# Loads of x issued two weight units apart, and a product of reciprocals that waits three units, in a hybrid encoder layer

## The chip, the cores and the metric

The kernel runs on one core of one Trainium2 chip. The metric is the device time of one execution in microseconds (us). Five engines run side by side, each in its own program order: TensorE (PE) multiplies matrices, VectorE (DVE) and ScalarE (ACT) work elementwise, GpSimd (POOL) takes a few additions, and SyncE (SP) issues most of the transfers (DMAs). An engine goes past an instruction only when the semaphores that it waits for have come.

## The reference

One encoder layer over x, 256 rows by 2048 columns in float32. Only its first steps matter here:

```python
h = rms_norm(x, norm1_g[i])       # x * rsqrt(mean(x*x) + eps) * g
proj = h @ w_in[i]                # 2048 x 20032: SSD z, xBC, dt | q, k, v | GLU | gates
y_ssd  = ssd_mixer(proj[..., COL_Z:COL_XBC], ..., dt = proj[..., COL_DT:COL_Q], ...) @ w_ssd_o[i]
y_att  = dilated_attention_mixer(q, k, v, q_norm_g[i], k_norm_g[i]) @ w_attn_o[i]   # q, k: RMSNorm per head
y_conv = conformer_conv(...) @ w_conv_o[i]
merged = sum over branches of sigmoid(gate) * y
x = x + merged @ w_out[i]
x = x + square(relu(rms_norm(x, norm2_g[i]) @ w_mlp_up[i])) @ w_mlp_down[i]
```

In the SSD branch `dt = softplus(dt_raw + dt_bias)`, and the decays are sums over the rows of `dt * a`.

## The kernel before

The weights are streamed once. They are cut into **blocks** (one output tile `main` each) and a block into **units** of 256 weight rows, mostly 8 to a block. For each unit the kernel loads the weights (`raw`, on SP's queue, five buffers), splits them into a high part `hi` (ACT, L1211) and a remainder `lo` (DVE, L255), and multiplies: high by high, high by the remainder of the activations, and `lo` by high (L1273, L1274, L1276 in one layout, L1264, L1266, L1268 in the other). In the program's order, loads stand five units ahead of the products (`load(k + 5)`), splits three (`LEAD`).

Units are counted from 0 here. Units 0 to 7 are block 0 (64 columns of dt and 384 of q), 8 to 15 block 1 (384 of k), 16 to 23 block 2 (384 of v). These three multiply `xg`, which is x times the gain, without the row's norm: the factor 1/rms is put on afterwards. From block 3 (unit 24, the first GLU block) on, the products use `h`, so they need `hh` and `hl`, the split of x times gain times 1/rms. There are two `main` tiles, so block n+2 may begin only once block n has been read.

Everything else is a set of **jobs**, Python generators that yield what they need, and a planner that puts their instructions between the units while it writes the program. `("w", n)` lets n units go by; `("v", cost)`, `("a", cost)`, `("p", cost)` ask for time on DVE, ACT and PE; `("m", n)` and `("b", n)` take buffers; `("j", test)` waits for another job. Priorities go from 0, the most urgent. After each unit, `tick` lets the jobs go on as far as their credits reach. Where a block needs something that isn't there yet, `require` forces the jobs, with no regard to credits and waits. From `mm` and from `Sched.require`:

```python
S.require(lambda: id(j) in st["main_free"], f"block {bi - 2} read")   # at the first unit of block bi
...
level = 0
while not cond():
    moved = False
    for j in [x for x in self.jobs if x.prio <= level]:
        while not cond() and not j.done and self._try(j, True):
            moved = True
```

What is forced is written ahead of the first product of the block that asked. The level rises only when no job of the lower levels can move.

The jobs of the first blocks:

- `job_rms1` (priority 0, added ahead of unit 3): loads x in its natural layout as four tiles `xr` of 512 KB (L318), sums the squares of each (ACT, L325), adds them up and takes the reciprocal of the root (`rstd_steps`: ACT L270, DVE L273 to L283) into `r`; `st["r1"]` then lets other jobs use it. `spread` puts `r` on a diagonal `dg` (DVE, L291), and a product with ones (PE, L296) spreads it over the partitions; DVE copies it to `rbc` (L338).
- `job_h` (priority 1): waits for `rbc`, and makes `hf`, `hh`, `hl` in four steps (DVE L354, ACT L357, DVE L255).
- `job_qk` (priority 0) for q of block 0 and k of block 1: squares of the heads (ACT, L459), then with `r` the norm of the heads (L469 to L482), the scaled copy `qn` (ACT, L489), transposes (PE, L501) and a copy out (ACT, L505, L506). For block 0, `main` counts as read only once this job has made `qn` and `job_dt` has read its columns.
- `job_dt` (priority 1) for block 0: waits for `r`, scales its 64 columns (DVE, L386), permutes the rows by a product (PE, L395), computes softplus as absolute value, exponential (ACT, L403, L404) and a series of small operations (DVE, L408 to L424), then a product that adds up the decays (PE, L436).

`job_rms2`, the second norm, also calls `spread`.

Of the kernel before, what the change touches and what calls it, by code (L numbers as in the profile page):

```python
# [190 lines left out]
def kernel(ctx: ExitStack, tc: tile.TileContext, xT, xn, par, cm, cd, cq, w1, wq, ws, out):  # L191
# [17 lines left out]
    def slab(shape, dt=F32, name="s"):  # L209
        return gp.tile([P] + list(shape), dt, tag="g", name=nm(name))  # L210

    def bank(shape=(512,), name="b"):
        return pd.tile([P] + list(shape), F32, tag="d", name=nm(name))

    def small(shape, name, dt=F32, bufs=None):
        return sm.tile([P] + list(shape), dt, tag=name, name=nm(name), bufs=bufs)
# [30 lines left out]
    def natural(ap):  # L247

        return ap.rearrange("p (j r) -> p r j", r=2)

    def strided(ap):
        return ap.rearrange("p (r j) -> p r j", r=2)
# [12 lines left out]
    def rstd_steps(dst, ms, n):  # L265

        s = small([n], f"rs{n}", bufs=2 if n < 64 else 1)
        r = small([n], f"rr{n}", bufs=2 if n < 64 else 1)
        yield "a", 1500 + n
        A.activation(s, ms, AF.Sqrt)  # L270
        yield "w", 1
        yield "v", (100 if n == T else 800) + 7 * n
        V.reciprocal(r, s)  # L273
        for b_ in (r, ms):
            if n == T:
                yield "v", 200 + n
            V.tensor_tensor(s, r if b_ is r else s, b_, op=ALU.mult)
        if n == T:
            yield "v", 200 + n
        V.tensor_scalar(s, s, -0.5, 1.5, op0=ALU.mult, op1=ALU.add)  # L280
        if n == T:
            yield "v", 200 + n
        V.tensor_tensor(dst, r, s, op=ALU.mult)  # L283

    def spread(r):

        yield "m", 1
        dg = slab([2, P], name="dg")
        yield "v", 400
        for t in range(2):  # L290
            V.tensor_scalar(dg[:, t, :], ID, r[:, t:t + 1], None, op0=ALU.mult)  # L291
        yield "w", 1
        yield "b", 1
        b = bank()
        yield "p", 440
        PE.matmul(b[:, :T], ones, dg, start=True, stop=True)  # L296
        S.give()
        yield "w", 1
        return b[:, :T]
# [10 lines left out]
    def job_rms1():  # L310

        xss = small([2, 2], "xss1", bufs=1)
        yield "m", 4
        xs_ = []
        for t in range(2):
            for e in range(2):
                xr = slab([1024], name="xr")
                nc.sync.dma_start(xr, xn.rearrange("(p t) d -> p t d", t=2)[:, t, e * 1024:e * 1024 + 1024])  # L318
                xs_.append(xr)
        yield "w", 2  # L320
        for t in range(2):
            for e in range(2):
                yield "a", 1300
                xr = xs_[2 * t + e]
                A.activation(xr, xr, AF.Square, accum_out=xss[:, t, e:e + 1])  # L325
        S.give(4)
        yield "w", 1
        m2 = small([2], "ms2", bufs=2)
        yield "v", 300
        V.tensor_reduce(m2, xss, axis=AX.X, op=ALU.add)  # L330
        V.tensor_scalar(m2, m2, 1.0 / D, EPS, op0=ALU.mult, op1=ALU.add)
        r2 = cp.tile([P, 2], F32, name="r2")
        yield from rstd_steps(r2, m2, 2)
        st["r1"] = r2
        b = yield from spread(r2)
        rbc = small([T], "rbc", bufs=1)
        yield "v", 400
        V.tensor_copy(natural(rbc), strided(b))  # L338
        S.banks += 1
        st["rbc1"] = rbc  # L340
# [676 lines left out]
    def job_rms2():  # L1017
        xss = small([2, 4], "xss", bufs=1)
        for i in range(4):
            yield "j", lambda: oacc[i] is not None  # L1020
            yield "m", 1
            sq = slab([2, 512], name="sq2")
            for t in range(2):
                yield "a", 650
                A.activation(sq[:, t, :], oacc[i][:, t, :], AF.Square, accum_out=xss[:, t, i:i + 1])
            S.give()
        ms = small([2], "ms2", bufs=2)
        yield "w", 1
        yield "v", 250
        V.tensor_reduce(ms, xss, axis=AX.X, op=ALU.add)  # L1030
        V.tensor_scalar(ms, ms, 1.0 / D, EPS, op0=ALU.mult, op1=ALU.add)
        r = small([2], "ry", bufs=1)
        yield from rstd_steps(r, ms, 2)
        b = yield from spread(r)
        rb = small([T], "rbc", bufs=1)
        yield "a", 300
        A.activation(rb, b, AF.Copy)
        S.banks += 1
        st["rbc2"] = rb
# [61 lines left out]
    def start_jobs():  # L1101
        S.add(job_rms1(), "rms1", 0)
# [298 lines left out]
```

## Time and profile before

| | |
|---|---|
| time, median of 3 runs | 1983.57 us (1982.33 to 1984.44) |
| the profiled execution: time | 1982.2 us |
| its span, first to last instruction | 1980.4 us |
| mean granted TensorE clock | 0.998 of full |
| PE busy | 1965.4 us (99% of the span) |
| DVE, ACT, POOL busy | 66%, 52%, 2% |
| HBM read | 360.45 MB, 183 GB/s over the span |

A row of the timeline gives start, duration, engine, line and operation, output from input, count, and in brackets the idle time ahead of it with what ended it. Busy PE time counts the ends of pipelined products, so the spacing of starts tells the pace. In the group rows stand count, total busy us, mean ns, and the engine's idle time before them. Names in the profile leave out the buffer numbers.

### The profile page before, as it was taken

What the parts mean: (1) busy time and instruction counts of PE and PEld (TensorE: products, weight loads), DVE (VectorE), ACT (ScalarE), POOL (GpSimd) and SP (SyncE); (2) the same over time, 40 slices, a digit from 0 to 9 for tenths busy, and PEclk for the clock granted to TensorE, in tenths of its full rate; (3) what the DMA queues carried; (4) which work ended last, traced back from release to release, by engine and by line L of the source; (5) the groups of instructions that cost most, each with busy time, mean ns of one, the idle gap of its engine ahead of it and who ended that gap; (6) DMA issues with size and microseconds to landing.
All of it is one profiled execution on the core that took longest, in us unless ns stands there. A gap on an engine that the chain in (4) does not pass through costs nothing.

```text
span 1980.4 us, 29949 instructions
## 1 busy us (share of the span) xinstructions
PE 1965.4 (99%) x11798; PEld 1766.0 (89%) x11798; DVE 1309.1 (66%) x1847; ACT 1036.5 (52%) x1446; POOL 47.4 (2%) x42
## 2 busy tenths in 40 slices
PE   8999999999999999999999999999999999999999
PEld 7999999999998888888888888999988998998887
DVE  5778987887887889896655555555555554455443
ACT  6555576777756655545654444544443443354332
POOL 0000010000000000003000000000000000000000
PEclk9999999999999999999999999999999999999999
DMA  8555564554555555555555556555555555555554
GB/s 289 184 173 190 163 186 142 169 173 141 180 169 167 174 181 181 181 191 186 188 190 189 184 193 207 195 183 190 192 190 189 186 191 191 190 185 190 191 181 149
DMA packets 105342, 364.51 MB, mean 184 GB/s; under 512 B 11760, under 2 KB 12272, under 8 KB 105200
## 3 DMA queue, kind: packets, MB, share of 16 engines
q1 hardware_dynamic: 103904, 360.23, 55.4%
q10 hardware_dynamic: 1296, 2.36, 0.3%
q8 instruction: 92, 1.51, 0.3%
q14 instruction: 50, 0.41, 0.1%
HBM read 360.45 MB, written 2.10 MB: 183 GB/s over the span
## 4 chain that ended last, share of the span: by engine, by line
PE 95%; DVE 0%; issue 0%
PE main L1273 19%; PE main L1274 19%; PE main L1276 19%; PE main L1266 11%; PE main L1264 11%; PE main L1268 11%; PE b L842 1%; PE b L864 1%; PE b L968 1%; PE b L1273 0%; PE b L1274 0%; PE b L1276 0%; PE b L819 0%; PE b L501 0%; PE b L757 0%; PE b L685 0%
## 5 line engine op out<-in xcount | busy, mean ns | idle before, releaser
L255 DVE TENSOR_TENSOR lo<-raw,hi 128x1024 fp32r<-128x1024 f32 (+2 forms) x697 | 831.5, 1194 | 643.7 <-ACT hi L1211 638.5
L1211 ACT ACTIVATE hi<-raw 128x1024 fp32r<-128x1024 f32 (+2 forms) x695 | 716.1, 1032 | 868.7 <-PE main L1274 487.0
L1273 PE MATMUL main<-hi,hh 128*128 128x512 f32 (+1 forms) x800 | 306.1, 383 | 0.0
L1274 PE MATMUL main<-hi,hl 128*128 128x512 f32 (+1 forms) x800 | 299.0, 374 | 0.0
L1266 PE MATMUL main<-x2l,hi 128*128 128x256 f32 x1024 | 246.4, 281 | 0.0
L1264 PE MATMUL main<-x2h,hi 128*128 128x256 f32 x1024 | 246.3, 279 | 0.0
L1266 PE MATMUL main<-hl,hi 128*128 128x256 f32 x896 | 216.3, 281 | 3.2 <-DVE hl L255 3.2
L1264 PE MATMUL main<-hh,hi 128*128 128x256 f32 x896 | 217.7, 282 | 0.0
L565 DVE SCALAR_TENSOR_TENSOR co<-cin,cpar,co 128x256 f32<-128x256 f32 x480 | 211.1, 491 | 0.0
L1276 PE MATMUL main<-lo,hh 128*128 128x512 f32 (+1 forms) x800 | 200.5, 372 | 0.0
L1264 PEld LDWEIGHTS main<-x2h,hi 128*128 128x128 f32 x1024 | 192.7, 188 | 0.2
L1266 PEld LDWEIGHTS main<-x2l,hi 128*128 128x128 f32 x1024 | 192.6, 188 | 0.2
L1273 PE MATMUL main<-hi,ah 128*128 128x512 f32 x480 | 188.9, 394 | 0.0
L1274 PE MATMUL main<-hi,al 128*128 128x512 f32 x480 | 188.6, 393 | 0.0
L1273 PEld LDWEIGHTS main<-hi,hh 128*128 128x128 f32 x800 | 152.5, 191 | 23.3 <-ACT hi L1211 1.2
L1274 PEld LDWEIGHTS main<-hi,hl 128*128 128x128 f32 x800 | 152.2, 190 | 22.9 <-issue 1.9
L1266 PEld LDWEIGHTS main<-hl,hi 128*128 128x128 f32 x896 | 168.8, 188 | 4.2 <-DVE hl L255 3.6
L1264 PEld LDWEIGHTS main<-hh,hi 128*128 128x128 f32 x896 | 169.2, 189 | 0.6
L1276 PEld LDWEIGHTS main<-lo,hh 128*128 128x128 f32 x800 | 148.0, 190 | 22.1
L1268 PE MATMUL main<-x2h,lo 128*128 128x256 f32 x1024 | 138.3, 277 | 0.0
L1276 PE MATMUL main<-lo,ah 128*128 128x512 f32 x480 | 130.1, 393 | 0.0
L1268 PEld LDWEIGHTS main<-x2h,lo 128*128 128x128 f32 x1024 | 127.6, 188 | 0.0
(244 smaller groups left out, 2303.8 us busy)
## 6 DMA issues: line engine op xcount, KB each, us to landing
raw<-ws_dram SPq DMA_DIRECT2D x600, 512.0 KB, 3.3
raw<-wq_dram SPq DMA_DIRECT2D x88, 384.0 KB, 3.1
raw<-w_dram SPq DMA_DIRECT2D x7, 448.0 KB, 7.1
xr<-xn_dram SPq DMA_DIRECT2D x4, 512.0 KB, 8.5
x<-xn_dram SPq DMA_DIRECT2D x4, 512.0 KB, 4.4
xt<-xT_dram SPq DMA_DIRECT2D x7, 256.0 KB, 7.2
out_dram<-x SPq DMA_DIRECT2D x4, 256.0 KB, 3.7
out_dram<-x ACTq DMA_DIRECT2D x4, 256.0 KB, 5.6
```

What stands on the lines that cost most here:

```text
L255: V.tensor_tensor(lo, raw, hi.bitcast(F32), op=ALU.subtract)
L565: V.scalar_tensor_tensor(dst[:, e, :], x[:, e, k:k + T], par_("dw", (2 * i + e) * 31 + k), dst[:, e, :], op0=ALU.mult, op1=ALU.add)
L842: PE.matmul(ba, lt, src, start=(n == 0), stop=(n == 3))
L864: PE.matmul(bd[:, i, :], em[:, 0, i, :], x[:, c, pr:pr + P], start=True, stop=True)
L968: PE.transpose(b[:, e, t * P:t * P + P], src[:, t, k * P:k * P + P], ID)
L1211: A.activation(h, r, AF.Copy)
L1264: PE.matmul(o, wh[:, e, cs], ah, start=(first and e == 0 and c % 2 == 0), stop=False, skip_group_check=True)
L1266: PE.matmul(o, wh[:, e, cs], al, start=False, stop=False, skip_group_check=True)
L1268: PE.matmul(o, wl[:, e, cs], ah, start=False, stop=(last and e == 1), skip_group_check=True)
L1273: PE.matmul(o, ah[:, xs_], wh[:, e, :], start=(first and e == 0), stop=False)
L1274: PE.matmul(o, al[:, xs_], wh[:, e, :], start=False, stop=False)
L1276: PE.matmul(o, ah[:, xs_], wl[:, e, :], start=False, stop=(last and e == 1))
```

## The change

In `job_rms1`, `yield "w", 2` stands after each of the four loads of x, where there was none; the wait of two units behind the loop stays. `spread` gets a parameter for the wait between the diagonal and its product, 1 as before by default, and 3 in the first norm. Lines below the edit move down by one.

```diff
-    def spread(r):
+    def spread(r, wait=1):
...
-        yield "w", 1
+        yield "w", wait
...
                 xs_.append(xr)
+                yield "w", 2
         yield "w", 2
...
-        b = yield from spread(r2)
+        b = yield from spread(r2, 3)
```

What the planner makes of it shows in the order of each engine's instructions. First SP's queue, where the loads of x meet the weight loads; `raw_228` is unit 8's weights, and the next `raw` rows are units 9, 10 and so on. Before:

```order
L1193 DMA raw_228<-wq_dram 128x768
L318 DMA xr_254<-xn_dram 128x1024
L318 DMA xr_256<-xn_dram 128x1024
L318 DMA xr_258<-xn_dram 128x1024
L318 DMA xr_260<-xn_dram 128x1024
L1193 DMA raw_262<-wq_dram 128x768
L1193 DMA raw_284<-wq_dram 128x768
```

The same place now:

```order
L1194 DMA raw_228<-wq_dram 128x768
L318 DMA xr_254<-xn_dram 128x1024
L1194 DMA raw_256<-wq_dram 128x768
L1194 DMA raw_278<-wq_dram 128x768
L318 DMA xr_296<-xn_dram 128x1024
L1194 DMA raw_298<-wq_dram 128x768
L1194 DMA raw_316<-wq_dram 128x768
L318 DMA xr_334<-xn_dram 128x1024
L1194 DMA raw_345<-wq_dram 128x768
L1194 DMA raw_378<-wq_dram 128x768
L318 DMA xr_396<-xn_dram 128x1024
```

The four loads of x stood in a row ahead of unit 9's weights; now two weight loads stand between each pair, and the last comes ahead of unit 15's.

Second, PE around the spread product (`dg` by ones, L296). Before, it stood between units 10 and 11, with `job_dt`'s first product behind it; `lo_326` is unit 10's remainder and `hi_356` unit 11's high part:

```order
L1276 MATMUL main_360<-lo_326,xgh_99 128x384 x4
L296 MATMUL b_430<-dg_405,ones 128x256
L395 MATMUL b_436<-dtt_342,perm_343 128x128 x4
L1273 MATMUL main_360<-hi_356,xgh_99 128x384
L1274 MATMUL main_360<-hi_356,xgl_102 128x384
```

Now it stands between unit 15 (`lo_437`) and unit 16 (`hi_454`, the first product into `main_679`, block 2):

```order
L1277 MATMUL main_354<-lo_437,xgh_101 128x384 x4
L296 MATMUL b_531<-dg_528,ones 128x256
L502 MATMUL b_590<-cmask,qn_582 128x128 x4
L502 MATMUL b_591<-cmask,qn_582 128x128 x2
L396 MATMUL b_639<-dtt_336,perm_337 128x128 x4
L437 MATMUL b_668<-adt,cmask 128x128 x4
L1274 MATMUL main_679<-hi_454,xgh_98 128x384
```

Four kinds of product moved to this one place: the spread product, the transposes of k's heads (`qn_582`; before they stood ahead of block 3), and `job_dt`'s permutation and its sums of decays (`adt`; before in block 4).

Third, ACT at the same place; `hi_511` is unit 19's split, `main_169` block 0, `main_354` block 1, `qn_549` q's heads. It read, before, from the first root on:

```order
L270 ACTIVATE rs_62_377<-ms_61_373 128x2
L1211 ACTIVATE hi_384<-raw_323 128x768
L459 ACTIVATE junk_381,ss_380<-main_169 128x128
L1211 ACTIVATE hi_414<-raw_351 128x768
L459 ACTIVATE junk_381,ss_380<-main_169 128x128 x4
L1211 ACTIVATE hi_443<-raw_382 128x768
L459 ACTIVATE junk_381,ss_380<-main_169 128x128
L1211 ACTIVATE hi_473<-raw_412 128x768
L270 ACTIVATE rs_88_493<-qms_462 128x6
L1211 ACTIVATE hi_499<-raw_441 128x768
```

And now, from the last split ahead of it:

```order
L1212 ACTIVATE hi_511<-raw_472 128x768
L326 ACTIVATE xr_396,xss_38_253<-xr_396 128x1024
L270 ACT_TABLE_LOAD
L270 ACTIVATE rs_91_520<-ms_90_516 128x2
L270 ACTIVATE rs_96_539<-qms_375 128x6
L490 ACTIVATE qn_549<-main_169,qrs_376 128x128 x6
L460 ACTIVATE junk_558,ss_557<-main_354 128x128 x6
L270 ACTIVATE rs_105_572<-qms_565 128x6
L490 ACTIVATE qn_582<-main_354,qrs_566 128x128 x6
L506 ACTIVATE qkT_583<-b_590,cpar 128x512
L507 ACTIVATE qkT_583<-b_591,cpar 128x256
L358 ACTIVATE hh_601<-hf_600 128x1024
```

Where weight splits alternated with steps of the jobs, the jobs' steps now follow each other; behind the last row shown come the other three `hh`, `job_dt`'s absolute value, its table load and its exponentials, and only then unit 20's split.

DVE's order has the same form: from unit 19's `lo` on, it has the first norm, both head norms, all of `hf` and `hl` and all of `job_dt` in one run, and then unit 20's `lo`. On every engine the order is the same as before again, row by row, from unit 57 to the end of the kernel.

## The prediction, made before the change was run

> **What bounds the kernel now.** I read the page's busy times first, then who made PE wait over the whole span, then PE's timeline over the first 150 us, where the change moves instructions.
>
> ```profile
> span 1980.4 us, 29949 instructions
> PE 1965.4 (99%) x11798; PEld 1766.0 (89%) x11798; DVE 1309.1 (66%) x1847; ACT 1036.5 (52%) x1446; POOL 47.4 (2%) x42
> PE main L1266 <- DVE hl L255: 3.2, 2, 2.2
> PE main L1273 <- ACT hi L1211: 2.6, 2, 2.2
> PE b L296 <- DVE dg L291: 2.6, 1, 2.6
> PE main L1273 <- ACT hi L1208: 1.5, 1, 1.5
> PE b L1288 <- DVE ones L236: 1.1, 1, 1.1
> ```
>
> PE is the bound: it stands idle for 15 us of 1980, and the five waits (us in total, times, longest) are all there are. The last two belong to the start. The other three, 8.4 us, lie in the first 90 us: all that better placing of this work can win, beside some time of a slow clock:
>
> ```profile
> 30.00:40.00 10.00, 6.26 (x25) 5.95 (x26) 5.64 (x16) 7.99 (x15) 0.00 (x0) 0.79 0.76 241
> ...
> 26.71 0.34 PE L1273 MATMUL main<-hi,xgh 128*128 128x384 f32 x1
> ...
> 31.19 0.45 PE L1273 MATMUL main<-hi,xgh 128*128 128x384 f32 x1 [2.22 <-ACT hi L1211]
> ...
> 34.22 0.52 PE L1273 MATMUL main<-hi,xgh 128*128 128x384 f32 x1
> 34.54 0.52 PE L1274 MATMUL main<-hi,xgl 128*128 128x384 f32 x1
> ...
> 39.77 1.22 PE L296 MATMUL b<-dg,ones 128*128 128x256 f32 x2 [2.55 <-DVE dg L291]
> ...
> 42.34 0.57 PE L1273 MATMUL main<-hi,xgh 128*128 128x384 f32 x1
> ...
> 44.69 0.34 PE L1273 MATMUL main<-hi,xgh 128*128 128x384 f32 x1
> ...
> 46.77 0.34 PE L1273 MATMUL main<-hi,xgh 128*128 128x384 f32 x1
> ...
> 53.09 0.45 PE L1273 MATMUL main<-hi,xgh 128*128 128x384 f32 x1
> ...
> 148.27 0.29 PE L1264 MATMUL main<-hh,hi 128*128 128x256 f32 x1
> ```
>
> These are the first products of units 8 (26.71), 9, 10, then the spread product, then units 11 (42.34), 12, 13, 16 (53.09) and 48 (148.27). An undisturbed unit of 384 columns takes 46.77 - 44.69 = 2.08 us, 12 products of 0.17. Unit 9 comes 2.2 us late, for its weights; unit 10 runs at 0.32 us a product (34.22 to 34.54), with a clock of 0.79 in that window; and PE stands 2.55 us before the spread product. So units 8 to 15 take 26.4 us (26.71 to 53.09) in place of 8 x 2.08 = 16.7.
>
> **The loads of x.** Why unit 9 is late:
>
> ```profile
> 15.01 5.04 SPq L318 DMA_DIRECT2D xr<-xn_dram  x4
> ...
> 30.30 0.84 ACT L1211 ACTIVATE hi<-raw 128x768 fp32r<-128x768 f32 x1 [3.46 <-DMA raw<-wq_dram]
> ...
> 20.00:30.00 10.00, 8.97 (x47) 8.35 (x45) 2.94 (x5) 3.91 (x6) 0.00 (x0) 1.00 1.03 402
> ```
>
> SP spends 5 us on the four loads of x, 2 MB, until 20.05; unit 9's weights come behind them, and ACT gets them at 30.30. After the change only one load of x, 0.5 MB, stands ahead of them. At the 402 GB/s that the window from 20 to 30 us moves, 1.5 MB less is 3.9 us earlier: 26.4, and with the split of 0.84 still ahead of 28.8, when unit 8 ends. From there each pair of units (4.2 us, 1.7 MB at that rate) needs two weight loads and a load of x, 1.3 MB. I cost the three later loads at nothing, covered by that margin; if it is gone, up to the 2.2 us of before come back. With no wait and no spread product in units 8 to 15, PE could start unit 16 at E = 26.7 + 16.7 = 43.4 instead of 53.09: 9.7 us won, 2.6 of them only because L296 and L395 (39.77 to 42.34) move away.
>
> **What stands before unit 16 now.** The loads end eight units later, the squares of x lie behind the splits of units 16 to 19, and `r` isn't there when block 2 asks for block 0's tile. So the planner forces the jobs, and writes out one after the other, ahead of unit 16: the rest of the first norm, q's head norm, k's, all of `job_h`, all of `job_dt`. PE's row in the order says that four kinds of product stand between units 15 and 16, so PE waits for the whole run, which before lay beside 80 us of products. Splits of units 16 to 19 are done; units 20 on are split behind the run, while PE has 8 us of work in hand, and weight loads up to unit 24 go on beside it, so nothing is late behind it. POOL isn't touched. Nor is the second norm, with its wait of 1. Prices of the run:
>
> ```profile
> 32.82 1.04 ACT L325 ACTIVATE xr<-xr 128x1024 f32<-128x1024 f32 x1
> L270 ACT ACT_TABLE_LOAD x1 | 1.3, 1283 | 0.0
> 38.24 0.16 DVE L273 RECIPROCAL rr<-rs 128x2 f32<-128x2 f32 x1
> L338 DVE COPY rbc<-b 128x256 f32<-128x256 f32 x1 | 0.4, 418 | 0.0
> 45.94 0.15 DVE L469 TENSOR_TENSOR r1sq<-r 128x2 f32<-128x2 f32 x1
> 46.73 0.21 ACT L270 ACTIVATE rs<-qms 128x6 f32<-128x6 f32 x1 [1.69 <-DVE qms L472]
> 60.31 0.18 DVE L273 RECIPROCAL rr<-rs 128x6 f32<-128x6 f32 x1
> 61.60 0.89 ACT L489 ACTIVATE qn<-main,qrs 128x128 f32<-128x128 f32 x3 [2.20 <-DVE qrs L482]
> 50.65 1.40 ACT L489 ACTIVATE qn<-main,qrs 128x128 f32<-128x128 f32 x5 [1.29 <-DVE qrs L482]
> 53.63 0.30 ACT L459 ACTIVATE junk<-main 128x128 f32<-128x128 f32 x1
> 55.84 0.20 ACT L459 ACTIVATION_READ_ACCUMULATOR junk<-main 128x1 f32 x1
> L506 ACT ACTIVATE qkT<-b,cpar 128x256 f32<-128x256 f32 x1 | 0.5, 462 | 0.0
> L357 ACT ACTIVATE hh<-hf 128x1024 fp32r<-128x1024 f32 x4 | 4.3, 1063 | 0.0
> L354 DVE SCALAR_TENSOR_TENSOR hf<-xt,cpar,rbc 128x256 f32<-128x256 f32 x16 | 7.1, 479 | 0.0
> L255 DVE TENSOR_TENSOR hl<-hf,hh 128x1024 fp32r<-128x1024 f32 x4 | 4.8, 1218 | 0.0
> 30.00:60.00 30.00, 1.91 (x8) 1.94 (x8) 0.83 (x4) 0.00 (x0) 0.89 0.63 200
> 60.00:72.00 12.00, 0.00 (x0) 0.00 (x0) 0.00 (x0) 0.66 (x2) 1.00 0.57 186
> 72.00:100.00 28.00, 0.00 (x0) 0.00 (x0) 5.11 (x16) 0.00 (x0) 1.00 0.56 178
> L436 PE MATMUL b<-adt,cmask 128*128 128x128 f32 x8 | 1.1, 275 | 0.0
> ```
>
> The three rows that begin with a window are the instructions of the tile `dtt` alone (PE, weight loads, DVE, ACT). In order, from E:
>
> - First norm to the spread product: 4.5 us. Unit 19's split needs unit 15's first eight products, so it starts 0.5 before E and takes 0.8; the last square 1.2 with the reading of its sum; the table load 1.3, which stands in ACT's order behind the squares; the root 0.2; from the reciprocal to the product 39.77 - 38.24 = 1.5.
> - Spread product 1.2 and its copy 0.4: 1.6.
> - q: from `r1sq` to the root's end 46.94 - 45.94 = 1.0; from the reciprocal to the first `qn` 61.60 - 60.31 = 1.3; six `qn` at 1.40/5, 1.7. Together 4.0.
> - k: its six squares stand behind q's copies on ACT: 53.63 to 56.04, 2.4; its mean and root 0.6 (the 1.0 less two small steps); 1.3; 1.7; transposes, of which only the last stay behind the copies, 0.3 (an estimate from the copies' pace); L506 0.5, L505 lying beside them. Together 6.8.
> - `job_h`: its first eight `hf` (3.5 us) lie beside k's copies and the first `hh`. On the path are one `hh` 1.1, four `hl` 4.8 and eight `hf` at 0.44, 3.5: 9.4.
> - `job_dt`: scaling and memset 0.55 (the 0.83 less 0.28 of L399), permutation 1.9, L399 0.3, absolute value and exponential 0.66 with a table load of 1.3, the series 5.1 and its last two steps 0.4, the sums of decays 1.1 at full clock (1.9 when slow, as the permutation was): 1.6. Together 11.8, with handoffs 0.3: 12.1.
>
> Sum: 4.5 + 1.6 + 4.0 + 6.8 + 9.4 + 12.1 = 38.4 us. Unit 16 starts at 43.4 + 38.4 = 81.8. From below, instructions that overlap with their follower by 0.05 to 0.1 us each over some 60 steps give 35; from above, 0.1 us more at each of some 30 handoffs gives 41.5. I take the sum as it stands, since its durations count overlaps and leave handoffs out, and these two go against each other.
>
> **The clock behind the run.** No row shows PE after a break of 38 us. The nearest is unit 9: after a break of 2.2 us products ran at 0.32 us instead of 0.17 until 35.8, 3.4 us, of which half is lost: 1.7. I take that, with ends 0 (the products of the run keep the clock up) and 3.4 (twice as long).
> The Trainium skill, "TensorE: Matmul & The Clock Gate", Part 1, says that TensorE goes to half clock after an idle window of about 3.4 us and comes back only after a busy one, with windows that run free of the kernel. The 3.4 us and the factor of two agree with the rows of units 9 and 10; by that rule unit 16 would start slow and lose between 1.7 and 3.4 us, so the sum would be up to 1.7 higher.
>
> **From unit 16 to unit 48.** Before, 148.27 - 53.09 = 95.2 us. The waits for `hl` (3.2) go, since `hl` is done, and so do k's transposes and the sums of decays (0.6 and 0.8 of start-to-start time, an estimate from 1.1 for the latter): 90.6. Unit 48 starts at 81.8 + 1.7 + 90.6 = 174.1, against 148.27. From unit 57 on each engine has its old order and PE has no wait left to shorten, so the 25.8 us stay to the end: 1982.2 + 25.8 = 2008.0 for the profiled execution. That one lies 1.4 below the median of the runs, so against the median the forecast is 1983.6 + 25.8, about 2009.
>
> **Rivals.**
> 1. Much slower than that: the handoffs or the clock cost more, as bounded above (3.1 and 1.7), and the weights are late again in spite of the spacing (2.2 and its slow clock 1.7). That gives up to 2018. For it speaks that DMA moved 402 GB/s when unit 9 was late; against it that x now goes out in quarters.
> 2. `job_dt` costs nothing: if its 12.1 us lay beside products, the time would be 1997. Its products stand ahead of unit 16 in PE's order, which speaks against it; only a start of `dt` ahead of `hl` would help, and DVE's order has it behind.
> 3. The other side, not slower: PE passes the products that wait and runs unit 16 as soon as its tile is free, which needs only the first norm and q's copies, 4.5 + 1.6 + 4.0 = 10.1. Then unit 48 starts at 43.4 + 10.1 + 92.0 = 145.5, where the products that wait still cost their 1.4, and the time is 1981, no more than 0.2% from before. It decides as soon as PE waits for less than about 12.6 us (148.27 - 1.7 - 90.6 - 43.4). Against it is the row at 39.77: unit 11's products had their operands, and PE stood for 2.55 us behind the product that waited.
> The same page of the Trainium skill, Part 2, step 1, says that matmuls stay in program order and only weight loads are pulled ahead; the row at 39.77 agrees.
>
> That the change doesn't reach the program is excluded by the order.
>
> **How the numbers follow.** The forecast's case gets 0.80, rival 1 gets 0.12, rival 2 gets 0.04, rival 3 gets 0.03, and 0.01 is left for a gain that I don't see. The predicted time is the first case's, 2009. Its own bounds, from the run (35 to 41.5) and the clock (0 to 3.4), give 2004 to 2014; the range goes to 2003 and 2015 and leaves out the end of rival 1 and the others. Slower by over 0.2%, about what a measurement of this kernel can tell from no change, holds in the first three: 0.96; rival 3 is 0.03 for the same; 0.01 for faster.
>
> **What would show it.** Right: no wait of PE for `hi` or `dg` in units 8 to 15; unit 16's first product near 82 us, with PE's waits ahead of it put down to `dg`, `qn`, `dtt` and `adt`, and over 30 us of idle time; a low clock in the windows from 45 to 85; no wait for `hl`; unit 48 near 174; from there the distance to before constant. Wrong: unit 9 late as before (the loads), unit 16 before 70 (the run is not in series), or a distance that shrinks after unit 48 (hidden slack behind the bound).

## The result, and the profile after

| | before | changed |
|---|---|---|
| time, median (us) | 1983.11 (1982.33 to 1984.44) | 2012.09 (2011.41 to 2012.63) |
| the profiled execution: time | 1982.2 | 2011.88 |
| its span | 1980.4 | 2010.1 |
| mean granted clock | 0.998 | 0.991 |

The change makes the kernel 29.0 us slower: ratio 1.0143, 95% interval 1.013 to 1.0156. The forecast was 25.8 more. Executions of one kernel differ by some us, together with the clock granted in them (the kernel before, over all its runs, from 1981.87 us at 0.999 to 1985.18 at 0.997), so a profiled execution can stand 1 to 3 us from its kernel's median. Read in the same order as before: the busy times of the page, then who made PE wait over the whole span (us in total, times, longest).

```profile
PE 1970.6 (98%) x11798; PEld 1770.1 (88%) x11798; DVE 1311.4 (65%) x1847; ACT 1038.0 (52%) x1446; POOL 47.4 (2%) x42
```

```profile
PE b L396 <- issue: 10.0, 1, 10.0
PE b L502 <- ACT qn L490: 9.2, 2, 8.9
PE b L437 <- DVE adt L425: 8.6, 1, 8.6
PE b L296 <- DVE dg L291: 4.3, 1, 4.3
```

PE stood idle for 15 us before. Four new waits make 32.1 us (10.0 + 9.2 + 8.6 + 4.3), and each is a wait of one of the four kinds of product that now stand between units 15 and 16. The waits for `hl` are gone. PE's timeline shows where they lie:

```profile
27.59 0.34 PE L1274 MATMUL main<-hi,xgh 128*128 128x384 f32 x1
29.68 0.34 PE L1274 MATMUL main<-hi,xgh 128*128 128x384 f32 x1
...
42.25 0.34 PE L1274 MATMUL main<-hi,xgh 128*128 128x384 f32 x1
...
48.81 1.22 PE L296 MATMUL b<-dg,ones 128*128 128x256 f32 x2 [4.30 <-DVE dg L291]
58.89 0.47 PE L502 MATMUL b<-cmask,qn 128*128 128x128 f32 x1 [8.86 <-ACT qn L490]
71.00 2.05 PE L396 MATMUL b<-dtt,perm 128*128 128x128 f32 x8 [10.01 <-issue]
81.63 2.04 PE L437 MATMUL b<-adt,cmask 128*128 128x128 f32 x8 [8.59 <-DVE adt L425]
83.33 0.67 PE L1274 MATMUL main<-hi,xgh 128*128 128x384 f32 x1
...
84.75 0.34 PE L1274 MATMUL main<-hi,xgh 128*128 128x384 f32 x1
...
173.73 0.28 PE L1265 MATMUL main<-hh,hi 128*128 128x256 f32 x1
```

Unit 8 starts at 27.59, unit 9 at 29.68, unit 15 at 42.25: seven steps of 2.09 us, none late. The relief of the weights that the loads were spaced for is real. Unit 16 then starts at 83.33, against 53.09 before, and unit 48 at 173.73, against 148.27. Where `issue` is named for L396, the records show no semaphore; the tile `dtt` comes from DVE, whose row is below. The steps of the run, on DVE and ACT (from r's square for q's heads, the squares of k's heads, the first `hh`, and the scaling of `dt`), and three windows inside it (PE, weight loads, DVE, ACT, POOL, then clock, share of DMA and GB/s):

```profile
50.41 0.15 DVE L470 TENSOR_TENSOR r1sq<-r 128x2 f32<-128x2 f32 x1
54.24 0.31 ACT L460 ACTIVATE junk<-main 128x128 f32<-128x128 f32 x1
61.54 2.00 ACT L358 ACTIVATE hh<-hf 128x1024 fp32r<-128x1024 f32 x2
70.42 0.47 DVE L387 TENSOR_SCALAR dtt<-main,r 128x64 f32<-128x64 f32 x2
```

```profile
50.00:60.00 10.00, 0.84 (x4) 0.52 (x4) 5.59 (x27) 5.70 (x26) 0.00 (x0) 0.50 0.00 0
60.00:70.00 10.00, 0.99 (x5) 0.59 (x3) 9.09 (x17) 5.18 (x7) 0.00 (x0) 0.50 0.00 0
70.00:80.00 10.00, 2.05 (x8) 1.78 (x8) 5.48 (x18) 2.05 (x4) 0.00 (x0) 0.50 0.00 0
```

For 30 us PE works 3.9, the DMA queues carry nothing, and the engines that do work take turns: this is a chain of dependent steps, at half the TensorE clock.

### The profile page after: what moved, and what is told of

It reads as the page before. It is cut to its first block, busy times and chain, and to the rows that moved or that the text cites. A ratio compares the mean times of both kernels' runs of the same rounds, so it can differ in the third digit from the quotient of the medians.

```text
span 2010.1 us, 29952 instructions
## 1 busy us (share of the span) xinstructions
PE 1970.6 (98%) x11798; PEld 1770.1 (88%) x11798; DVE 1311.4 (65%) x1847; ACT 1038.0 (52%) x1446; POOL 47.4 (2%) x42
## 4 chain that ended last, share of the span: by engine, by line
PE 98%; issue 1%; DVE 1%; ACT 1%; DMA 0%; SPq 0%; DVEq 0%
PE main L1274 20%; PE main L1275 20%; PE main L1277 19%; PE main L1265 11%; PE main L1269 11%; PE main L1267 11%; PE b L843 1%; PE b L865 1%; PE b L969 1%; PE b L1274 0%; PE b L1277 0%; PE b L1275 0%; PE b L820 0%; DMA raw<-w_dram 0%; PE b L502 0%
```

## The experiments

Times are compared with runs of the kernel before on the same chip: 1983.6 us (runs 1 to 4), 1983.8 (5 to 8), 1983.5 (9, 10), 1983.8 (11, 12). U16, U24, U32 and U48 are the starts of those units' first products in the profiled execution, "late part" the time from unit 441 to unit 687.

| kernel | time | ratio, 95% interval | U16 | U24 | U32 | U48 | late part |
|---|---|---|---|---|---|---|---|
| before | 1983.6 | | 53.09 | 71.22 | 99.37 | 148.27 | 685.84 |
| changed | 2012.09 | 1.013 to 1.0156 | 83.33 | 101.48 | 125.79 | 173.73 | 690.85 |
| 1 wait_only | 1988.99 | 1.0018 to 1.004 | 51.63 | 69.08 | 104.34 | 152.53 | 689.66 |
| 2 one_apart | 1998.09 | 1.0056 to 1.009 | 53.88 | 75.02 | 111.15 | 159.89 | 686.66 |
| 3 dt_read_only | 2017.75 | 1.0157 to 1.0187 | 54.34 | 85.40 | 131.05 | 179.89 | 687.49 |
| 4 placed_13 | 2011.23 | 1.0123 to 1.0153 | 83.53 | 102.06 | 126.37 | 174.31 | 689.74 |
| 5 one_load | 1980.18 | 0.9976 to 0.9994 | 48.45 | 66.56 | 94.67 | 143.45 | 689.84 |
| 6 start2_together | 1988.01 | 1.0016 to 1.0034 | 54.77 | 72.30 | 100.26 | 148.29 | 690.18 |
| 7 start1_together | 1986.86 | 1.0008 to 1.0026 | 57.18 | 74.62 | 100.72 | 148.64 | 689.25 |
| 8 start0_one_apart | 1984.30 | 0.9992 to 1.001 | 55.60 | 73.23 | 97.94 | 146.66 | 688.14 |
| 9 x_once | 1986.20 | 1.0005 to 1.0024 | 48.76 | 69.30 | 99.77 | 148.44 | 690.39 |
| 10 x_once_later | 2004.93 | 1.0094 to 1.0122 | 76.67 | 95.75 | 120.17 | 168.15 | 688.15 |
| 11 x_later_dt_read | 1989.61 | 1.0017 to 1.0036 | 46.87 | 64.98 | 99.17 | 148.01 | 688.33 |
| 12 x_once_credit | 1976.75 | 0.9954 to 0.9979 | 50.12 | 70.80 | 95.98 | 143.64 | 688.59 |

### The two parts of the change, and the forced run

The first theory, A: the run ahead of unit 16 is the whole loss, and whatever keeps the jobs from being forced there keeps the gain in units 8 to 15. **1, wait_only** has the loads together, as before, and only the wait of 3:

```diff
-        b = yield from spread(r2)
+        b = yield from spread(r2, 3)
```

> The second part of the change alone: the four loads of x in a row as before, the spread product three units behind the diagonal. Here the wait has an effect on the order: the product stands behind unit 12 and job_dt's permutation behind unit 11, and nothing is forced ahead of unit 16. Theory A (the run ahead of unit 16, made by the late loads, is the whole loss): no run, unit 9 late as before (about 2.2 us), no wait of PE for dg behind unit 10, unit 48 within 4 us of the 148.3 of before, time 1978 to 1987. Rival B (the later product itself costs, since rbc, hf and hl come two units later and block 3 waits for hl): PE waits for hl longer than the 3.2 us of before by two units, 4 us, and the time is 1985 to 1990.

Measured 1988.99, inside rival B's range. PE's longest wait, and the copy of the spread reciprocals on DVE, here and then in before:

```profile
PE main L1266 <- DVE hl L255: 5.5, 3, 2.5
```

```profile
47.13 0.42 DVE L338 COPY rbc<-b 128x256 f32<-128x256 f32 x1
```

```profile
43.40 0.42 DVE L338 COPY rbc<-b 128x256 f32<-128x256 f32 x1
```

PE no longer stands before the spread product and unit 16 is 1.5 us earlier, but `rbc` is copied 3.7 us later, and U24 to U32 takes 35.3 us where it took 28.2. The wait for `hl` is only 2.3 us longer than before, not the 4 of rival B. The granted clock of that stretch, the third number from the end, adds to it, 0.90 here and then 1.00 in before:

```profile
69.08:104.34 35.26, 29.79 (x219) 29.02 (x219) 25.24 (x44) 16.57 (x21) 0.00 (x0) 0.90 0.45 158
```

```profile
71.22:99.37 28.15, 24.94 (x207) 24.43 (x206) 23.71 (x44) 13.14 (x17) 0.00 (x0) 1.00 0.55 175
```

The clock can account for at most 0.10 x 35.3 = 3.5 us (an estimate from this row). The time saved at one product comes back at `h`, as waits and as a slower clock around them.

**2, one_apart** is the changed kernel with one unit between the loads:

```diff
-                yield "w", 2
+                yield "w", 1
```

> The loads of x one unit apart in place of two, the wait of three units kept. The order puts the spread product behind unit 15, but only q's head norm is forced ahead of unit 16; k's norm, job_h and the series of job_dt lie between later units. Theory A (a run is paid in full, what lies between units is not): no wait for weights in units 8 to 15, PE stands about 4 us ahead of unit 16 for q's norm, unit 16 near 48.7, unit 48 near 146, time 1977 to 1986, no slower than before. Rival B (late loads as such cost, by late h): unit 48 above 155 and time above 1990.

Measured 1998.09: rival B again. The weights of units 8 to 15 are in time, as in the changed kernel, and ahead of unit 16 only the first norm and q's copies are waited for; yet half of the loss is there.

```profile
PE main L1267 <- DVE hl L255: 8.1, 3, 3.9
PE main L1274 <- ACT qn L490: 6.4, 1, 6.4
```

**3, dt_read_only** is the changed kernel with `job_dt` cut in two, so that only its reading of block 0 has priority 0 and the rest need not be written ahead of unit 16:

```diff
         st["dt_read"] = True
+
+    def job_dt_rest():
+        yield "j", lambda: "dt_read" in st
...
-            return ([(job_dt(m), 1)] if j == 0 else []) + ...
+            return ([(job_dt(m), 0), (job_dt_rest(), 1)] if j == 0 else []) + ...
```

> The changed kernel, with job_dt cut in two: only the reading of its 64 columns keeps priority 0, the rest is a job of its own with priority 1. Then block 0 counts as read after the first norm, the spread product, the reading and q's norm; k's norm, job_h and the rest of job_dt are no longer forced ahead of unit 16. Theory A (PE waits for the sum of the run): the run falls from 39.0 to about 10.5 us (4.5 + 1.6 + 0.6 + 3.8), so unit 16 starts near 55; a second, shorter run of about 8 us appears ahead of unit 24, where k's copies, v and the first step of h are forced; time 1990 to 2001. Rival B (the loss is not the run, but lies with the late r or the slow clock): unit 16 above 70 and time above 2005.

Unit 16 starts at 54.34, as theory A expected, 29 us earlier than in the changed kernel; the time is 2017.75, 5.7 us longer. Theory A falls by the time, and rival B by unit 16, which it had above 70: with `r` as late as here, lifting the forced run moves the loss and doesn't remove it.

```profile
PE main L1273 <- DVE hl L255: 11.3, 4, 4.1
PE b L508 <- ACT qn L496: 5.4, 2, 5.1
PE main L1280 <- ACT qn L496: 4.8, 1, 4.8
PE b L296 <- DVE dg L291: 4.3, 1, 4.3
PE main L1271 <- ACT hh L358: 2.6, 1, 2.6
PE main L1280 <- DVE cin L544: 1.9, 1, 1.9
```

The work that isn't forced ahead of unit 16 is waited for later instead: U16 to U24 takes 31.1 us (18.1 in before) and U24 to U32 45.7 (28.2).

Spacing the loads and leaving the wait at 1 was not run: the order of every engine is then the same, row by row, as in the changed kernel. So the wait of 3 adds nothing to the spaced loads; with the loads together it costs 5.4 us.

**4, placed_13** asks for the last 4 to 5 us, which the changed kernel loses after unit 441, where both kernels have the same order. It moves the tiles made from the second norm's `x2` to other places, with an extra tile, of which POOL writes one column, in two of the four steps:

```diff
+        pads = [slab([4, T], name="pad") for _ in range(1)] if i in (1, 3) else []
+        for pad in pads:
+            G.memset(pad[:, 0, 0:1], 0.0)
```

> The changed kernel with the same instructions on PE, ACT, DVE and SP in the same order; GpSimd writes one column of an extra tile ahead of the second and the fourth output block, and again behind it, which moves the tiles x2h and x2l of these and the third block to other places in SBUF. The first block's stay. Theory A (the 4.2 us that the changed kernel loses between unit 449 and unit 661 come from where these tiles lie): units of the up products on the first tile keep their 2.79 us within 0.01, those on the other three leave their 2.844, 2.817 and 2.853 by more than 0.01, and the time moves by 30 times the sum of these changes, somewhere between 2004 and 2014. Rival B (the slower pace belongs to the execution or to what came ahead of it): all four keep their pace, time 2011 to 2013.

A unit of the MLP's up blocks took, by the tile of `x2` that it reads, 2.787, 2.807, 2.773 and 2.807 us in before, 2.789, 2.844, 2.817 and 2.853 in the changed kernel, and 2.795, 2.845, 2.813 and 2.827 here. The last three tiles have moved; two of them kept their pace and one came down by 0.026, so their place alone doesn't set it.

### How late `r` is

The next theory, L: the loss follows how late `r` comes, and the relief of the weights is worth something by itself. Its rival S: what is won in units 8 to 15 comes back later. **5, one_load** makes only the first load of x; the three other squares read that tile again, so the kernel leaves out three quarters of x in the norm and its result differs:

```diff
-                nc.sync.dma_start(xr, ...)
+                if not xs_:
+                    nc.sync.dma_start(xr, ...)
...
-        for t in range(2):
-            for e in range(2):
+        for t in (1, 0):
+            for e in (1, 0):
...
-                A.activation(xr, xr, AF.Square, accum_out=xss[:, t, e:e + 1])
+                A.activation(xr, xs_[0], AF.Square, accum_out=xss[:, t, e:e + 1])
```

> As before, but only the first of the four loads of x for the mean square is made; the other three squares read that tile again, so the mean square is that of a quarter of x (the result differs, the instructions stay). It takes 1.5 MB out of the way of unit 9's weights without making r later. Theory L (the change loses because r, 1/rms, comes later than blocks 2 and 3 can bear, and the relief of the weights is worth something by itself): unit 9 starts at its pace of 2.1 us behind unit 8 (28.8, before 31.2), rbc is copied at 43.4 or earlier, units 8 to 15 take 20 to 24 us (before 26.4), time 1976 to 1981. Rival S (the weights of unit 9 were late for nothing in the end, since the same time comes back as a longer wait for hl): unit 16 earlier by 2 us or more but unit 48 within 1 us of before's 148.3, time 1982 to 1985.

Theory L: unit 9 at 29.65, 2.1 us behind unit 8; `rbc` copied at 38.79; units 8 to 15 in 20.9 us (48.45 - 27.55); U48 4.8 us earlier than before; 1980.18. So 1.5 MB less beside the weights, with the earlier `r` that comes of it, is worth about 5 us at unit 48. Part of that is clock: the mean granted over units 8 to 15 is 1.00 here and 0.87 in before.

**6 to 8** look for an earlier `r` with all of x, and start the job ahead of unit 2, 1 or 0; the last has the loads one unit apart and the wait of 1.

```diff
-        if k == 3:
+        if k == 2:          # 1 in start1_together, 0 in start0_one_apart
             start_jobs()
+        if k == 3:
             nc.scalar.dma_start(cpar[:, 16:], par[:, 16:])
```

> As before (loads together, wait of 1), but the job of the first norm starts one unit earlier (ahead of unit 2, not 3), so that the spread product stands behind unit 9. Theory L: r comes 2 to 4 us earlier (rbc copied at 39.5 to 41.5, before 43.4), the waits for hl (3.2 us) shrink by 1.5 or more, time 1979 to 1982. Rival S: the 2 MB of x now stand ahead of unit 8's weights, unit 8 comes 2 to 4 us late instead of unit 9, and nothing is won: 1983 to 1987.

> As before, but the job of the first norm starts two units earlier (ahead of unit 1), the spread product stands behind unit 8. Theory L: rbc copied at 37 to 40.5, no wait for hl, time 1977 to 1981. Rival S: the 2 MB of x stand ahead of unit 7's weights, unit 7 comes 2 to 4 us late, time 1983 to 1988.

> Loads of x one unit apart as in the kernel that had them one apart, but the job starts three units earlier (ahead of unit 0) and the spread product waits 1 unit: it stands behind unit 11, as it did with the loads together and a wait of 3. Theory L: no unit of 8 to 11 waits for weights, the spread product itself delays nobody, rbc is copied at 44 to 47.5, and the time lies between before and the kernel with the wait of 3 alone (1989.0), less the relief of the weights: 1981 to 1987. Rival S (spacing the loads costs by itself): 1989 to 1998, as the kernel with the loads one apart (1998.1).

Measured 1988.01, 1986.86 and 1984.30. For the first two rival S is right (the first is 1 us past its range): the 2 MB only meet other weights, and `rbc` comes only 0.7 and 1.4 us earlier. PE's waits of the three kernels, in that order:

```profile
PE b L296 <- DVE dg L291: 4.4, 1, 4.4
PE main L1273 <- ACT hi L1211: 1.9, 1, 1.9
```

```profile
PE main L1273 <- ACT hi L1211: 5.3, 2, 5.0
PE b L296 <- DVE dg L291: 2.0, 1, 2.0
```

```profile
PE b L296 <- DVE dg L291: 4.0, 1, 4.0
PE main L1274 <- ACT hi L1212: 2.8, 4, 1.4
```

In start0_one_apart the weights are late four times by a little (theory L had none) and the spread product still waits 4.0 us; unit 48 is 1.6 us earlier than before, and the time is within what can be told from no change.

### x read once

**9, x_once** takes the natural x out altogether. The squares come from the transposed x, which is on the chip for block 0 anyway, and 16 products with a tile of 1/2048 add them up over the partitions:

```diff
-                nc.sync.dma_start(xr, ...)
...
+        for i in range(4):
...
+            sq = slab([4, T], F32R, name="xsq")
+            A.activation(sq, xt[i], AF.Square)
...
+        yield "w", 1
+        yield "b", 1
+        b = bank()
+        for k in range(KC):
+            PE.matmul(b[:, :T], onesdr, xsq[k // 4][:, k % 4, :], start=k == 0, stop=k == KC - 1)
...
+        yield from rstd_steps(rbc, ms, T)
...
+            V.tensor_tensor(dg[:, t, :], rbc[:, t:T:2], ID, op=ALU.mult)
+        V.tensor_reduce(r2, dg, axis=AX.X, op=ALU.add)
```

> The natural copy of x isn't loaded at all (2 MB less in units 8 to 15). The squares are taken from the transposed x that block 0 multiplies anyway (ACT, four of 128x1024), 16 products with a tile of 1/2048 add them up over the partitions behind unit 6 (about 1.9 us of PE at 0.117 each), and 1/rms comes out spread over the partitions; r in the other layout is its diagonal. Theory D (what before loses in units 8 to 16 is that 2 MB of x, the weights and an early r can't all be had; one_load won 3.7 us of it with 1.5 MB less): no unit waits for weights or dg, rbc is there by 36, unit 16 starts at 45 to 48 (before 53.1), unit 48 at 137 to 141 (before 148.3), time 1972 to 1979, the late drift of 0 to 5 us included. Rival P (the planner gives the won time back as waits for qn, hl or dtt at units 16 to 30, as it did when the job was merely started earlier): unit 48 at 144 or later, time 1981 or more.

Theory D was nearly right up to unit 16 and wrong behind it; the time, 1986.20, is rival P's. `rbc` is ready at 36.4 (35.93 and 0.43), no unit from 8 to 15 is late, and unit 16 starts 4.3 us earlier than before:

```profile
35.93 0.43 DVE L283 TENSOR_TENSOR rbc<-rr,rs 128x256 f32<-128x256 f32 x1
```

But U16 to U24 takes 20.5 us (18.1 before), U24 to U32 30.5 (28.2), and unit 48 is where it was. Up to 3.5 of these 4.7 us (an estimate, 0.08 x 20.5 + 0.06 x 30.5) go with a slower clock, 0.92 over U16 to U24 and 0.94 over U24 to U32, where before has 1.00 in both:

```profile
69.30:99.77 30.47, 26.76 (x207) 26.06 (x206) 22.04 (x40) 12.05 (x14) 0.00 (x0) 0.94 0.46 154
```

Here `rbc` is 7.5 us earlier on the chip than in before (36.36 against 43.82), `r` itself only 1.0 us (38.21 against 39.19), and 2 MB less are loaded; together this buys nothing. Even the shortest of its eleven executions, 1984.49 us, is above before's median, so theory L falls as it stood.

**10, x_once_later** waits one unit more ahead of the 16 products (`yield "w", 2`). That is enough for the planner to force the jobs ahead of unit 16.

> As x_once, with the 16 products one unit later, behind unit 7. r is still earlier than in before, yet the planner now forces job_dt to its end ahead of unit 16 (the permutation and the sums of decays stand between units 15 and 16), as in the changed kernel. Theory F (a forced job costs its length whatever r does: the run of job_dt took 12.9 us in the changed kernel): unit 16 comes 8 to 13 us later than in x_once, time 8 to 13 us longer than x_once's. Rival G (only a late r makes the run long; with r early DVE and ACT have done most of it by then): within 4 us of x_once.

Theory F by direction, but past its range: 18.7 us longer than x_once, where 8 to 13 were expected. `r` is there at 39.55, no earlier than in before (39.19; `rbc` at 37.71 against 43.82), while unit 15 ends at 45.7 (43.61 + 2.09); still PE waits for three of the four kinds of product, and unit 16 starts at 76.67:

```profile
39.13 0.42 DVE L345 TENSOR_REDUCE r<-dg 128x2 f32<-128x256 f32 x1
52.28 0.47 PE L509 MATMUL b<-cmask,qn 128*128 128x128 f32 x1 [6.41 <-ACT qn L497]
```

```profile
PE b L403 <- issue: 10.0, 1, 10.0
PE b L444 <- DVE adt L432: 8.5, 1, 8.5
PE b L509 <- ACT qn L497: 6.7, 2, 6.4
```

The first two waits are those of the changed kernel to 0.1 us. The run is 31.0 us here, not the 12.9 of `job_dt` alone, and 39.0 there; what is missing is the first norm (6.1) and some 2 us of q's (the transposes start 6.6 us behind unit 15, 52.28 - 45.7; in the changed kernel 8.5 behind the first norm, 58.89 - 50.41).

**11, x_later_dt_read** is x_once_later with the edit of dt_read_only.

> As x_once_later, with job_dt cut in two so that only its reading of block 0 has priority 0 (the edit of the kernel dt_read_only, now with an early r). Theory F (what costs the time is that whole jobs are forced ahead of unit 16; where r stands early enough in the program, lifting the force gives the time back): unit 16 at 46 to 50 (76.7 in x_once_later), unit 48 at 146 to 152, time 1983 to 1991. Rival K (as in dt_read_only, the work that isn't forced ahead of unit 16 comes back as waits ahead of units 24 to 31): unit 16 early all the same, unit 48 at 158 or later, time 1996 or more.

Theory F: unit 16 at 46.87, unit 48 at 148.01, 1989.61. With kernels 3 and 10 it makes a square:

| | jobs forced ahead of unit 16 | force lifted |
|---|---|---|
| `r` behind the last spaced load | 2012.1 | 2017.8 |
| `r` early in the program | 2004.9 | 1989.6 |

The early `r` alone gives 7.2 us, the lifted force alone costs 5.7, and both together give 22.5: with `r` early in the program, lifting the force gives 15.3. The rows of the square also differ in the loads of x and in how `r` is made, but no unit from 9 to 15 is late in any of the four kernels. I read this as: what counts is how many units lie between `r` and the block that needs the last of its work (block 3 at unit 24), and whether the planner may use them. Two places of `r` don't show how the loss grows with that number.

**12, x_once_credit** tests why x_once gave its early `r` back. The jobs get credit for DVE and ACT from unit to unit; at units 8 to 23 it is raised by half:

```diff
-        S.tick({"v": ... * VSHARE, "a": ... * ASHARE, ...})
+        b_ = 1.5 if 8 <= k < 24 else 1.0
+        S.tick({"v": ... * VSHARE * b_, "a": ... * ASHARE * b_, ...})
```

> As x_once, with half as much again of credit on DVE and ACT for the jobs at units 8 to 23, so that the planner writes hf and hl earlier (the first hl ahead of unit 17's splits' end, three of four parts ahead of block 3). Theory C (in x_once the early r is given back because the planner's credits hold h back until block 3: 24 to 32 took 30.5 us there, 28.2 in before, and units without waits take 22.7): 24 to 32 takes 27 us or less, unit 48 at 141 to 146, time 1978 to 1984. Rival X (the jobs then hold up the splits on DVE or ACT): PE waits 3 us or more for hi or lo in units 9 to 23, unit 24 at 71 or later, time 1986 or more.

Theory C: U24 to U32 25.2 us, unit 48 at 143.64, and 1976.75, a little better than its range. It is the only complete version here that beats both kernels, by 0.34% (0.21% to 0.46%) before and 35.3 us the changed one. Of the 7.1 us against before, 4.6 are there at unit 48; no run separates the rest, which lies behind it. The raised credit alone, in the kernel before, was not run, so its share isn't known apart from the loads. The wait for `hl` is gone from PE's list, which now begins with the tile `dtt` of `job_dt`, the next thing to bring forward:

```profile
PE main L1281 <- DVE dtt L395: 3.8, 1, 3.8
```

## Why the prediction was right, and where it was not

**The loads.** Right. No unit from 8 to 15 is late. Unit 16 could have started at E = 44.3 (42.25 + 2.09), where 43.4 was forecast; the 0.9 us are there at unit 1 already (10.41, in before 9.54), at the start of the program.

**The run.** Right, term by term, with the rows above: to the spread product 48.81 - 44.3 = 4.5 (forecast 4.5); product and copy 50.41 - 48.81 = 1.6 (1.6); q 54.24 - 50.41 = 3.8 (4.0); k 61.54 - 54.24 = 7.3 (6.8); `job_h` 70.42 - 61.54 = 8.9 (9.4); `job_dt` 83.33 - 70.42 = 12.9 (12.1). Sum 39.0, forecast 38.4. Overlaps and handoffs did cancel. (The lower bound of the run was worked out loosely: 0.05 to 0.1 us at each of 60 steps takes 3 to 6 us off 38.4 and gives 32.4 to 35.4, not 35.) Rival 2 (`job_dt` for nothing) and rival 3 (PE passes what waits) are excluded by the four waits; of rival 1, the late weights are excluded by unit 9.

**The clock behind the run.** Mis-sized: 0.75 us, not 1.7 (unit 16 took 2.83 us where a unit takes 2.08). Products have their full pace from 84.75 on, 3.1 us after `adt`'s began at 81.63; so the run's own last products had done more than half of the slow stretch. That it is so small here has luck in it. The same eight products stand ahead of unit 16 in placed_13 and in x_once_later; there unit 16 took 3.20 and 3.74 us, so it lost 1.1 and 1.7, and the clock came back 3.9 and 5.1 us after these products began. In x_once_later:

```profile
74.94 2.07 PE L444 MATMUL b<-adt,cmask 128*128 128x128 f32 x8 [8.50 <-DVE adt L432]
...
80.41 0.34 PE L1281 MATMUL main<-hi,xgh 128*128 128x384 f32 x1
```

```profile
74.94:80.08 5.14, 5.14 (x19) 5.14 (x20) 0.66 (x3) 1.22 (x6) 0.00 (x0) 0.50 0.00 0
```

In the records of each of the 14 traces the granted clock changes only at moments that are whole multiples of 3.41 us apart (in the changed kernel from 47.19 to 84.74, eleven of them), so the loss depends on where in such a step these products fall. The row that the term was taken from shows it too. In before, products came 0.17 to 0.18 us apart from 31.48 to 32.37, right behind the break, and 0.32 apart only from 32.62 to 35.82: the slow 3.4 us are a whole step, not the time right behind the break, as the prediction read it. The Trainium skill, "TensorE: Matmul & The Clock Gate", Part 1, says that the activity is watched in a free-running window of 3413 ns; the steps of 3.41 us agree, and so does the spread from 3.1 to 5.1 us. The 1.7 to 3.4 us that the prediction worked out by that page were for a unit with nothing ahead of it.

**From unit 16 to unit 48.** 90.4 us with the clock in it, forecast 92.3. Unit 48 at 173.73, forecast 174.1: the distance to before there is 25.5 us, where 25.8 was predicted. That this is so close is partly luck: unit 16 came 1.5 us later than forecast (0.9 at the start, 0.6 in the run), and the stretch behind it was 1.9 us shorter (0.95 of it the clock).

**"The 25.8 us stay to the end."** This step failed. Units 441 and 687 of before, then of the changed kernel:

```profile
1265.24 0.28 PE L1264 MATMUL main<-x2h,hi 128*128 128x256 f32 x1
1951.08 0.40 PE L1273 MATMUL main<-hi,ah 128*128 128x512 f32 x1
```

```profile
1289.98 0.28 PE L1265 MATMUL main<-x2h,hi 128*128 128x256 f32 x1
1980.83 0.40 PE L1274 MATMUL main<-hi,ah 128*128 128x512 f32 x1
```

The distance is 24.7 us at unit 441 and 29.75 at unit 687. It grows by 0.02 to 0.03 us a unit, in every up block (2.794 us a unit before, 2.826 now) and a little in the down blocks. PE has no wait there, and the clock is 1.00 in both, as in this window over the same units (before, then changed, 27.4 us later; the columns as above). The changed kernel gets through 427 products in it where before gets through 432:

```profile
1550.00:1600.00 50.00, 50.00 (x432) 50.00 (x432) 27.01 (x25) 22.80 (x22) 0.00 (x0) 1.00 0.58 190
```

```profile
1577.40:1627.40 50.00, 50.00 (x427) 50.00 (x426) 26.48 (x24) 22.75 (x22) 0.00 (x0) 1.00 0.57 189
```

In the up blocks 0.022 of the 0.032 lie in the eight products with `lo`, 0.918 us for the eight before and 0.940 now. I took for granted that the same instructions in the same order take the same time; here they differ by 1.1% in the up blocks. All thirteen other kernels of the table have a longer late part than before (686.7 to 690.9 us against 685.8), so before's execution is the one that ran it fast, and up to 5 us of any comparison with it come from there. One execution of each kernel was traced, so whether the pace belongs to the kernel or to the execution isn't shown; for the kernel speaks that the changed kernel and kernel 4 agree within 0.006 us in three of the four tiles. Kernel 4 speaks against the place of `x2`'s tiles as the cause; what the cause is stays open. At the median the change costs 3.2 us more than the 25.8 that were forecast; the predicted range had room for that, but for other reasons.

**What made `r` late matter.** The prediction read it from the order, and that was enough for the number. The experiments add what it did not say: the run is not the cause by itself. With `r` late and the run lifted the time was 5.7 us longer, and units 24 to 31 (block 3, which needs the same work) alone took 17.5 us more than in before; with `r` early the same lift gave 15.3 us.

## What to carry to other kernels

A planner that forces unfinished jobs when a tile is due turns a small delay in the program into a chain of dependent steps with TensorE idle: before moving a value later, find every point that needs its work, count the units that are left for it, and price the chain from the rows of the steps, which here came within 0.6 us in 39. Relieving a queue can be worth nothing while the work behind it is held back elsewhere: among the complete versions here, only the one with the bytes removed and the credit raised together beat the kernel before. When TensorE waits in several places, price the slower clock around each wait as well as the wait. And compare late stretches of the trace, not only the place of the change: the same order ran 0.7% faster in one traced execution than in another.

## What the hardware showed that I had not expected

- Equal instructions in equal order had a pace of 2.794 or 2.826 us a unit, steady over all 15 up blocks after unit 441, with no wait and a clock of 1.00.
- The granted clock went to 0.50 for the run's three windows, 30 us with 3.9 us of PE work in them, though products were issued in each: a few products every 10 us didn't hold the clock.
- All changes of the granted clock lie whole multiples of 3.41 us apart in each of the 14 traces. The same products ahead of the same unit left it a loss of 0.75, 1.1 or 1.7 us, and a wait of 1.9 us for the tile `cin`, which four kernels have, was followed by 3.41 us at a clock of 0.50 in one_apart (from 584.19) and x_later_dt_read (from 573.01), where it lay inside one step, and by none in x_once and dt_read_only, where it lay across two.
- One solid run of waits cost less here than waits spread over the units. In dt_read_only PE's waits were no longer in sum (30.3 us in six groups against 32.1 in four), but the clock stayed low among them and units ran slowly in between: 0.69 and 0.71 in these windows, where the changed kernel, its run behind it, had 0.88 and 1.00.

```profile
80.00:100.00 20.00, 11.61 (x61) 10.43 (x62) 8.32 (x14) 8.71 (x15) 0.00 (x0) 0.69 0.23 80
100.00:120.00 20.00, 15.88 (x94) 15.45 (x93) 6.39 (x8) 6.17 (x8) 0.00 (x0) 0.71 0.16 53
```
